# An encoder block on one core: the inverse spread over its group, norms' sums after the next projection, a fourth pair of weight buffers

## The chip, the cores and the metric

The kernel runs on one core of a Trainium2 chip. The core has TensorE (PE, matmuls, with its weight loads as PEld), VectorE (DVE), ScalarE (ACT), GpSimd (POOL) and SyncE (SP), each with its own instruction stream, and DMA queues. The metric is the device time of one execution in microseconds (us). A measurement is the median of several executions; the profile is taken on one execution of its own.

## The reference

One layer of a hybrid encoder on 512 tokens of width 1024, all in float32. The input is normalized, projected by one wide matrix, and the columns feed three token mixers: a short gated convolution (a), a gated linear recurrence (b), and RWKV-7 time mixing with 16 heads of 64 (c). Their gated sum goes through an output projection, then comes a squared-ReLU MLP of width 4096 and a last norm.

```python
h = rms_norm(x, norm1_g[l])
p = h @ w_in[l]
pa, pb, pg, pc = _split(p, (COLS_A, COLS_B, COLS_GATE, COLS_C))
...
kk = kk / jnp.maximum(jnp.sqrt(jnp.sum(kk * kk, axis=-1, keepdims=True)), 1e-12)
k = k * (1.0 + (a - 1.0) * rwkv_ka[l])
...
yc = rwkv7_recurrence(rh, decay.reshape(hs), kh, vh, kk, ah)
...
m = gate_a * y_a + gate_b * y_b + gate_c * y_c
x = x + m @ w_out[l]
h2 = rms_norm(x, norm2_g[l])
x = x + jnp.square(jax.nn.relu(h2 @ mlp_w1[l])) @ mlp_w2[l]
```

The recurrence runs over the tokens one by one in the reference. The kernel does it in 8 chunks of 64 tokens, for which it needs, per chunk and head, the inverse of a unit triangular 64 x 64 matrix.

## The kernel before

**Numbers.** A float32 operand of a large matmul is split into a high and a low part in the fp32r type: ACT casts the high part, DVE subtracts it from the source for the low part (`split_w` for weights, `split` for others, both through the helpers on lines 147 and 104). A product is then three matmuls, high x high, high x low, low x high (`mm3`, lines 168 to 170).

**Weights.** `load_w` loads 128 x 1024 weights by a DMA of SP into `raw` (2 buffers) and splits them into `whi` and `wlo`, a pair that has 3 buffers. It does so at a raised priority (`OFF`). A projection (`proj`) is 24 matmuls of 512 columns on one such pair, with a yield after each six but the last.

**Order.** The framework that builds the program orders each engine's instructions by priority (program order, unless `high_priority` raises it), with a model of their times. `keep_in_program_order` fixes an instruction's place, and `pin` raises small matmuls far up and fixes them. Each engine then runs its instructions in the order built. The waits between engines are put in by the framework. The order across stages is written by hand with generators: `weave(crit, fill, r)` runs one step of a critical generator, then r steps of a filler.

**Stages.**
- A prologue: norm sums, the first three projections on unnormalized data, `pro_scale`, which makes `hh` and `hl`.
- Four groups g of four heads each. `krv` computes k, r, v and the decays for a group: for each of two column blocks the k projection, a token shift, the squares `sq` and their split `b`, the norms' sums `pn` (two matmuls against a block matrix `bd`), `rsqrt_rows`, which makes `kk`, then the r projection and the rest. `amat` makes the chunk matrices. `inverse` makes the triangular inverses on DVE: two transposes (L551), 31 elimination steps of two operations each (a product into `dg`, an addition into `Z`), two transposes (L573), one more (L578), and then matmuls of 32 x 32 blocks, `pG` and `pT`. The inverse of group g - 1 is woven with `fill_group(g)`: 22 steps of the filler `ab`, then `krv(g)` with 16 steps of `ab` spread among its own, then 4 more. Factor `R1` sets how many filler steps go with one step of the inverse; what is left of the group runs after it. `N_TT`, `NINV` and `NG_T` are empty steps of the inverse (yields) around its transposes and small matmuls. The last inverse is woven with `ab` alone, by `R2`.
- The chain over 8 chunks (`chain`), with `ab`, `gate` and the merge of the first half (`fin_m(0, 4)`) as its filler; then `end`: `fin_m(4, 8)`. `fin_m` makes tiles `ym` in DVE, casts them on ACT and subtracts for the low part.
- The output projection, `to_tokens` (transposes `tp`, a copy `st` on DVE, a sum of squares on ACT with a scratch output `sj`), the MLP and the final norm.

`ab(q)` computes mixers a and b for one block of 128 columns: eight projections with elementwise work on DVE and ACT in between. `gate(q)` does one projection and the gate of mixer c, with a tile tagged `gc`.

Of the kernel before, what the change touches and what calls it, by code (L numbers as in the profile page):

```python
# [9 lines left out]
F32 = mybir.dt.float32  # L10
# [11 lines left out]
CP, CPV, CPI, CPC, CPN = 150, 20, 0, 20, 5  # L22
HOT = 6000

N_TT, NINV, NG_T, N_LOAD = 2, 7, 4, 6


N_KRV = 22
F_INV, F_KRV, F_GAP = 22, 16, 4
W3 = 3  # L30
R0, R1, R2, R3, R4 = 0.85, 0.87, 0.9, 1.7, 1.0
NWARM = 2
POOL_KT = (1, 3, 5, 6, 7)
S = 512
# [64 lines left out]
def block_kernel(ctx, tc, xt, win, par, mulr, sw, wout, w1, w2, fg, cst, eyes, out):  # L99
# [39 lines left out]

    def new_w():  # L140
        return (wp.tile([P, D], F32, tag="raw", name="raw", bufs=2),
                wp.tile([P, D], F32R, tag="whi", name="whi", bufs=3, align_bytes=AL),
                wp.tile([P, D], F32R, tag="wlo", name="wlo", bufs=3, align_bytes=AL))

    def split_w(w, sl):
        raw, hi, lo = w
# [40 lines left out]
            stt(t, t, -0.5, y, MUL, MUL)  # L187
            stt(y, t, 1.5, y, ADD, MUL)

    def rsqrt_rows(pool, o, ps, low, scale=1.0):  # L190

        w = pool.tile([P, S], F32, tag="rqw", name="rqw")
        q = pool.tile([P, 3, 16], F32, tag="rqq", name="rqq")
        v.transpose(w, ps)
        wv = w.rearrange("p (b j) -> p b j", j=32)[:, :, 0]
        if scale == 1.0:
            v.tensor_scalar(out=q[:, 0], in0=wv, scalar1=low, scalar2=None, op0=MAX)
        else:
            ts2(q[:, 0], wv, scale, low, MUL, ADD)
        rsqrt(q[:, 0], q[:, 1], q[:, 2])  # L200
        v.transpose(o, q[:, 1].unsqueeze(2).to_broadcast([P, 16, 32]))
# [214 lines left out]
    def krv(g, G_):  # L416
        G_.AR = pk.tile([P, 2, NC, 2, L], F32, tag="AR", name="AR")
        G_.BK = pk.tile([P, 2, NC, 2, L], F32, tag="BK", name="BK")
        vs = [p1.tile([P, S], F32, tag=f"v{h}", name=f"v{h}") for h in range(2)]
        for jj in range(2):  # L420
            j = 2 * g + jj
            rs = WP("rs")
            if j == 0:
                ks = k0
            else:
                ks = WP("ks")
                t = yield from proj(("k", j))
                shift(t, pv("mu_k", j), dvp(OMK, j), ks)
            sq = WP("a1")
            ac.activation(sq, ks, AF.Square, scale=pv("kk", j))  # L430
            sqh, sql = split(pk, sq, "b")
            pn = pm.tile([P, S], F32, tag="pm", name="pn")
            pe.matmul(pn, bd, sqh, start=True, stop=False)
            pe.matmul(pn, bd, sql, start=False, stop=True)
            kk = WP("a5")
            rsqrt_rows(pk, kk, pn, 1e-24)
            stt(kk, ks, pv("kk", j), kk, MUL, MUL)
            yield
            t = yield from proj(("r", j))
            shift(t, pv("mu_r", j), dvp(OMR, j), rs)  # L440
            yield
            swh, swl = load_sw(pk, "swa", j, 0, 2)
            pw = pm.tile([P, S], F32, tag="pm", name="pw")
            pe.matmul(pw, swh[:, 0], lws, start=True, stop=False)
            pe.matmul(pw, swl[:, 0], lws, start=False, stop=True)
            sig = WP("a1")
            ac.activation(sig, pw, AF.Tanh, bias=pv("w0", j), scale=0.5)
            v.tensor_scalar(out=sig, in0=sig, scalar1=1.0, scalar2=None, op0=ADD)
            pa = pm.tile([P, S], F32, tag="pm", name="pa")
            pe.matmul(pa, swh[:, 1], las, start=True, stop=False)  # L450
            pe.matmul(pa, swl[:, 1], las, start=False, stop=True)
            av = WP("a4")
            ac.activation(av, pa, AF.Tanh, bias=pv("a0", j), scale=0.5)
            cum = WP("a2")
            v.tensor_tensor_scan(out=cum, data0=smk, data1=sig, initial=0.0, op0=MUL, op1=ADD)
            PP = pk.tile([P, NC, L + 1], F32, tag="PPt", name="PPt")
            gp.memset(PP[:, :, 0:1], 1.0)
            Pt = PP[:, :, 1:L + 1]
            ac.activation(Pt, c3(cum), AF.Exp, scale=-0.5 * CW)
            v.tensor_copy(PL[:, g, jj], PP[:, :, L])  # L460
            pinv = WP("a3")
            ac.activation(pinv, cum, AF.Exp, scale=0.5 * CW)
            stt(G_.AR[:, jj, :, 0], c3(kk), -1.0, PP[:, :, 0:L], MUL, MUL)
            tt(G_.AR[:, jj, :, 1], c3(rs), Pt, MUL)
            t_ = WP("a1")
            stt(t_, av, 1.0, kk, ADD, MUL)
            stt(G_.BK[:, jj, :, 0], c3(t_), 0.5, c3(pinv), MUL, MUL)
            kp = WP("a2")
            ts2(kp, av, pv("ka", j), dvp(OKA, j), MUL, ADD)
            tt(kp, kp, ks, MUL)  # L470
            tt(G_.BK[:, jj, :, 1], c3(kp), c3(pinv), MUL)

            if jj == 0:
                rk = [WP(f"rk{h}") for h in range(2)]
            for h in range(2):
                r = slice(64 * h, 64 * h + 64)
                stt(rk[h][64 * jj:64 * jj + 64], rs[r], part[r, PI["rk"], j:j + 1], kp[r], MUL, MUL)

        for jj in range(2):
            for h in range(2):  # L480
                gp.dma_start(axd[:, 0:64, g, 0, 2 * h + jj].rearrange("c d t -> d c t"),
                             G_.AR[64 * h:64 * h + 64, jj, :, 0])
            gp.dma_start(rtd[:, :, g, jj].rearrange("c p t -> p c t"), G_.AR[:, jj, :, 1])
        rk = [split(pk, rk[h], ("a1", "a3") if h else "b") for h in range(2)]
        for h in range(2):
            q = 2 * g + h
            t = yield from proj(("v", q))
            shift(t, pv("mu_v", q), dvp(OMV, q), vs[h])
            yield
        for h in range(2):  # L490
            pb = pm.tile([P, S], F32, tag="pm", name="pb")
            for i in range(2):
                pe.matmul(pb, bd, rk[h][i], start=i == 0, stop=i == 1)
            BV[2 * g + h] = [bv_tile(2 * g + h, th) for th in range(2)]
            for th in range(2):
                tt(BV[2 * g + h][th], pb[:, HALF[th]], vs[h][:, HALF[th]], MUL)
        yield
        for b in range(2):
            pt = pm.tile([P, 2, 2, P], F32, tag="pm", name="pV")
            for i in range(2):  # L500
                for h in range(2):
                    pe.transpose(pt[:, i, h], vs[h][:, (2 * b + i) * P:(2 * b + i + 1) * P], ident)
            vt = p1.tile([P, 2, 2, P], F32, tag="vt", name="vt", bufs=2)
            ac.copy(vt, pt)
            for i in range(2):
                c = 2 * (2 * b + i)
                gp.dma_start(vtd[c:c + 2, :, g].rearrange("c s e v -> (c s) (e v)"),
                             vt[:, i].rearrange("p h x -> p (h x)"))
        yield
# [34 lines left out]
    def inverse(g, G_):  # L544
# [12 lines left out]
        for s in range(31):  # L557
            n, c = 31 - s, s + 1
            tv = tmp[:, 0:n * c].rearrange("l (c t) -> l c t", c=c)
            mm = tt(tv, la[:, s, s + 1:32].unsqueeze(1).to_broadcast([64, c, n]),  # L560
                    xt[:, 0:c, s:s + 1].to_broadcast([64, c, n]), MUL)
            if s % 6 == 5:

                tc.keep_in_program_order(mm)
            tt(xt[:, 0:c, s + 1:32], xt[:, 0:c, s + 1:32], tv, ADD)
            yield
# [139 lines left out]
    def fin_m(c_lo, c_hi):  # L706

        n, th = c_hi - c_lo, c_lo // 4
        for g in range(NG):
            pt = pm.tile([P, 4, P], F32, tag="pm", name="pYt")  # L710
            for i in range(n):
                pe.transpose(pt[:, i], C["Y"][:, c_lo + i, 2 * g:2 * g + 2].rearrange("p j v -> p (j v)"), ident)
            for h in range(2):
                q = 2 * g + h
                y = C["ph2"].tile([P, HT], F32, tag="ym", name="ym", bufs=2)
                tt(y.rearrange("p (c t) -> p c t", t=L), pt[:, 0:n, 64 * h:64 * h + 64],
                   GQ[q][th].rearrange("p (c t) -> p c t", t=L), MUL)
                tt(y, y, BV[q][th], ADD)
                GQ[q][th], BV[q][th] = gq_tile(q, th, F32R), bv_tile(q, th, F32R)
                ac.copy(GQ[q][th], y)  # L720
                tt(BV[q][th], y, f(GQ[q][th]), SUB)
            yield

    def gate(q):

        yc = wk.tile([P, S], F32, tag="g3", name="yc")
        gp.dma_start(yc, mpd[q])
        gt = wk.tile([P, S], F32, tag="gc", name="gc")
        t = yield from proj(("gc", q))
        ac.activation(gt, t, AF.Tanh, bias=pv("mgc", q), scale=0.5)  # L730
        swh, swl = load_sw(wk, "swc", q, 4, 1)
# [201 lines left out]
    def to_tokens(th):  # L933
        for i in (2 * th, 2 * th + 1):
            for half in range(2):
# [4 lines left out]
                st = M["xrp"].tile([P, S], F32, tag="st", name="st", bufs=2)  # L940
                v.tensor_copy(st, tp)
                gp.dma_start(x2d[i, :, half * S:(half + 1) * S], st)
                sj = M["xrp"].tile([P, S], F32, tag="sj", name="sj")
                ac.activation(sj, tp, AF.Square, accum_out=ss2[:, half, i:i + 1])
                yield

    def end():
# [181 lines left out]
```

## Time and profile before

| | us |
|---|---|
| runs shown, median of 3 (lowest to highest) | 1108.27 (1107.01 to 1110.66) |
| the profiled execution | 1108.38 |
| its span | 1106.6 |
| elimination steps of the first inverse, first to last start of `dg` | 114.2 to 155.6 |
| of the second | 234.7 to 297.9 |
| of the third | 363.1 to 412.4 |
| of the last | 485.5 to 537.0 |

In the profile an engine's busy time is the time in which it has an instruction under way. PE's matmuls are pipelined, so a PE that is busy all the time can still run below its rate: the count of matmuls in a stretch and the granted clock (PEclk) tell that. In a row of the time line the numbers are start, duration, engine, line and operation, with the idle time ahead of it and what ended it in square brackets. Rows of groups give the count, the busy time and the mean duration in ns, then the idle time ahead; rows of a tile give the count and the durations as lowest, median and highest. Rows of waits give who waited for whom, the total in us, how often, and the longest. Many elementwise operations stand on the lines of the helpers (L104, L107, L110, L147, L163), so they are told apart by their tiles.

### The profile page before, as it was taken

To read this page: it belongs to the slowest core of one execution; us is meant where nothing else is said; L and a number is where in the kernel's file an instruction comes from. 1 tells how busy PE (TensorE), PEld (TensorE's weight loads), DVE (VectorE), ACT (ScalarE), POOL (GpSimd) and SP (SyncE) were. 2 spreads that over 40 slices of the span, in tenths; PEclk is the share of its full clock that TensorE was granted. 3 is DMA by queue.
4 is the path that set the end of the run, shared out by engine and by line. 5 is a ranking of instruction groups with operands and counts; after the bars stand their busy time and mean duration, and the time that the engine had idled before them with its cause. 6 is when DMAs were issued, how large, how long until landed. Compare 5 with 4: busy or idle time off the path is not lost.

```text
span 1106.6 us, 16112 instructions
## 1 busy us (share of the span) xinstructions
PE 1056.1 (95%) x6396; PEld 865.3 (78%) x6396; DVE 743.6 (67%) x1276; ACT 473.9 (43%) x698; POOL 108.9 (10%) x167
## 2 busy tenths in 40 slices
PE   8899979999799989999899999999999999999996
PEld 5677868887588867887687887898888888888885
DVE  7997898879978998769947677955444443222224
ACT  6655445454344534534555444334433333221114
POOL 3211000210011101210022220001000000000001
PEclk9899989999989989999999999999999999999999
DMA  6243623562234623553279773234333335322231
GB/s 209 83 124 98 180 79 113 139 182 86 77 105 129 177 85 96 147 148 106 79 225 281 263 223 101 87 124 153 96 99 98 104 99 191 96 95 95 96 95 76
DMA packets 43324, 142.13 MB, mean 128 GB/s; under 512 B 5681, under 2 KB 9265, under 8 KB 42225
## 3 DMA queue, kind: packets, MB, share of 16 engines
q1 hardware_dynamic: 29472, 91.02, 25.7%
q0 software_dynamic: 13056, 49.03, 15.9%
q8 instruction: 50, 0.82, 0.3%
q10 hardware_dynamic: 720, 1.05, 0.3%
q14 instruction: 26, 0.20, 0.1%
HBM read 115.91 MB, written 25.17 MB: 127 GB/s over the span
## 4 chain that ended last, share of the span: by engine, by line
PE 65%; DVE 21%; DMA 5%; issue 5%; ACT 3%; POOL 1%; SPq 0%; ACTq 0%; POOLq 0%; DVEq 0%
PE pp L168 8%; PE pp L169 7%; PE pp L170 7%; PE acc L170 6%; PE acc L168 6%; PE acc L169 6%; PE p L169 5%; PE p L168 5%; PE p L170 5%; DVE wlo L104 4%; DMA raw<-in_win 3%; DVE dg L104 2%; DVE Z L104 2%; DMA rt<-rtd 1%; DVE u L107 1%
## 5 line engine op out<-in xcount | busy, mean ns | idle before, releaser
L104 DVE TENSOR_TENSOR wlo<-raw,whi 128x1024 fp32r<-128x1024 f32 (+1 forms) x164 | 199.5, 1219 | 249.8 <-ACT whi L147 248.9
L147 ACT CAST whi<-raw 128x1024 fp32r<-128x1024 f32 (+1 forms) x164 | 169.6, 1036 | 326.9 <-PE acc L170 125.1
L168 PE MATMUL pp<-hh,whi 128*128 128x512 f32 x696 | 278.5, 401 | 7.2 <-DVE ks L107 4.6
L170 PE MATMUL pp<-hh,wlo 128*128 128x512 f32 x696 | 277.5, 399 | 7.6 <-DVE wlo L104 7.6
L169 PE MATMUL pp<-hl,whi 128*128 128x512 f32 x696 | 277.4, 399 | 2.8 <-DVE hl L107 2.8
L168 PEld LDWEIGHTS pp<-hh,whi 128*128 128x128 f32 x696 | 133.7, 192 | 38.6 <-DVE ks L107 5.0
L170 PEld LDWEIGHTS pp<-hh,wlo 128*128 128x128 f32 x696 | 133.8, 192 | 37.6 <-DVE wlo L104 9.6
L169 PEld LDWEIGHTS pp<-hl,whi 128*128 128x128 f32 x696 | 133.7, 192 | 30.9 <-DVE hl L107 3.2
L170 PE MATMUL p<-h2h,wlo 128*128 128x512 f32 (+1 forms) x264 | 101.4, 384 | 0.0
L168 PE MATMUL p<-h2h,whi 128*128 128x512 f32 (+1 forms) x264 | 101.3, 384 | 0.0
L169 PE MATMUL p<-h2l,whi 128*128 128x512 f32 (+1 forms) x264 | 101.1, 383 | 0.0
L168 PE MATMUL acc<-whi,ah 128*128 128x512 f32 x256 | 99.6, 389 | 0.0
L169 PE MATMUL acc<-wlo,ah 128*128 128x512 f32 x256 | 99.6, 389 | 0.0
L170 PE MATMUL acc<-whi,al 128*128 128x512 f32 x256 | 99.6, 389 | 0.0
L168 PEld LDWEIGHTS p<-h2h,whi 128*128 128x128 f32 x264 | 49.7, 188 | 9.6
L170 PEld LDWEIGHTS p<-h2h,wlo 128*128 128x128 f32 x264 | 49.6, 188 | 9.7
L169 PEld LDWEIGHTS p<-h2l,whi 128*128 128x128 f32 x264 | 49.6, 188 | 9.5
L170 PEld LDWEIGHTS acc<-whi,al 128*128 128x128 f32 x256 | 48.0, 188 | 10.1
L169 PEld LDWEIGHTS acc<-wlo,ah 128*128 128x128 f32 x256 | 48.0, 188 | 10.0
L168 PEld LDWEIGHTS acc<-whi,ah 128*128 128x128 f32 x256 | 48.0, 188 | 9.8
L104 DVE TENSOR_TENSOR Z<-Z,dg 64x31 f32<-64x31 f32 (+15 forms) x124 | 42.2, 340 | 4.1
L104 DVE TENSOR_TENSOR dg<-Z 64x31 f32<-64x31 f32 (+15 forms) x124 | 42.2, 340 | 4.0
(296 smaller groups left out, 1457.0 us busy)
## 6 DMA issues: line engine op xcount, KB each, us to landing
raw<-in_win SPq DMA_DIRECT2D x88, 512.0 KB, 3.6
raw<-in_w SPq DMA_DIRECT2D x64, 512.0 KB, 3.5
ax<-axd POOLq DMA_DIRECT2D x8, 1024.0 KB, 7.2
axd<-AXt POOLq DMA_DIRECT2D x12, 512.0 KB, 7.2
bkd<-BKT POOLq DMA_DIRECT2D x4, 1024.0 KB, 13.6
raw<-in_wout SPq DMA_DIRECT2D x8, 512.0 KB, 4.3
bk<-bkd POOLq DMA_DIRECT2D x7, 512.0 KB, 8.0
swr<-in_sw SPq DMA_DIRECT2D x16, 128.0 KB, 2.3
```

The lines of the kernel that those rows point to most:

```text
L104: return v.tensor_tensor(out=o, in0=a, in1=b, op=op)
L107: return v.scalar_tensor_tensor(out=o, in0=a, scalar=s, in1=b, op0=op0, op1=op1)
L147: ac.copy(hi[:, sl], raw[:, sl])
L168: pe.matmul(ps, wh, xh, start=start, stop=False)
L169: pe.matmul(ps, wh, xl, start=False, stop=False)
L170: pe.matmul(ps, wl, xh, start=False, stop=stop)
```

## The change

Seven edits:
- The inverse's empty steps go from `N_TT, NINV, NG_T` = 2, 7, 4 to 1, 4, 3, so it yields 47 times where it yielded 54. `R1` goes from 0.87 to 1.2 and `R2` from 0.9 to 1.02.
- Every third elimination step is kept in program order, where it was every sixth.
- In `krv` the two matmuls of `pn`, `rsqrt_rows` and `kk` stand after the r projection and its shift; the square and its split stay where they were.
- `whi` and `wlo` get 4 buffers each.
- `rsqrt_rows` in `krv` uses the tile tagged `a3` for its transposed input.
- `ym` has one buffer, the gate's tile is `g1` or `g2` by turns, `sj` is gone.
- The Square of `to_tokens` is written back over its own input `tp`.

```diff
-N_TT, NINV, NG_T, N_LOAD = 2, 7, 4, 6
+N_TT, NINV, NG_T, N_LOAD = 1, 4, 3, 6
...
-R0, R1, R2, R3, R4 = 0.85, 0.87, 0.9, 1.7, 1.0
+R0, R1, R2, R3, R4 = 0.85, 1.2, 1.02, 1.7, 1.0
...
-                wp.tile([P, D], F32R, tag="whi", name="whi", bufs=3, align_bytes=AL),
-                wp.tile([P, D], F32R, tag="wlo", name="wlo", bufs=3, align_bytes=AL))
+                wp.tile([P, D], F32R, tag="whi", name="whi", bufs=4, align_bytes=AL),
+                wp.tile([P, D], F32R, tag="wlo", name="wlo", bufs=4, align_bytes=AL))
...
-    def rsqrt_rows(pool, o, ps, low, scale=1.0):
+    def rsqrt_rows(pool, o, ps, low, scale=1.0, tag="rqw"):
 
-        w = pool.tile([P, S], F32, tag="rqw", name="rqw")
+        w = pool.tile([P, S], F32, tag=tag, name="rqw")
...
             sqh, sql = split(pk, sq, "b")
+            yield
+            t = yield from proj(("r", j))
+            shift(t, pv("mu_r", j), dvp(OMR, j), rs)
             pn = pm.tile([P, S], F32, tag="pm", name="pn")
             pe.matmul(pn, bd, sqh, start=True, stop=False)
             pe.matmul(pn, bd, sql, start=False, stop=True)
             kk = WP("a5")
-            rsqrt_rows(pk, kk, pn, 1e-24)
+            rsqrt_rows(pk, kk, pn, 1e-24, tag="a3")
             stt(kk, ks, pv("kk", j), kk, MUL, MUL)
-            yield
-            t = yield from proj(("r", j))
-            shift(t, pv("mu_r", j), dvp(OMR, j), rs)
             yield
...
-            if s % 6 == 5:
+            if s % 3 == 2:
 
                 tc.keep_in_program_order(mm)
...
-                y = C["ph2"].tile([P, HT], F32, tag="ym", name="ym", bufs=2)
+                y = C["ph2"].tile([P, HT], F32, tag="ym", name="ym", bufs=1)
...
-        gt = wk.tile([P, S], F32, tag="gc", name="gc")
+        gt = W(f"g{1 + q % 2}")
...
-                sj = M["xrp"].tile([P, S], F32, tag="sj", name="sj")
-                ac.activation(sj, tp, AF.Square, accum_out=ss2[:, half, i:i + 1])
+                ac.activation(tp, tp, AF.Square, accum_out=ss2[:, half, i:i + 1])
```

## The prediction

> **What bounds the kernel now.** The first view is the page: the span, the busy time of each engine, the forty slices and the chain that ended last.
>
> ```profile
> span 1106.6 us, 16112 instructions
> PE 1056.1 (95%) x6396; PEld 865.3 (78%) x6396; DVE 743.6 (67%) x1276; ACT 473.9 (43%) x698; POOL 108.9 (10%) x167
> PE   8899979999799989999899999999999999999996
> DVE  7997898879978998769947677955444443222224
> PEclk9899989999989989999999999999999999999999
> PE 65%; DVE 21%; DMA 5%; issue 5%; ACT 3%; POOL 1%; SPq 0%; ACTq 0%; POOLq 0%; DVEq 0%
> ```
>
> PE is the resource, but VectorE holds a fifth of the chain, and the digits say where: up to slice 20 (about 560 us) PE drops below 9 in those slices in which DVE shows 8 or 9. After that PE stays full. So the second view is the table by stretches: the three whole groups, the last inverse, the chunk chain, and two stretches of 20 us. A row gives start and end, the length, the busy time of PE, of its weight loads, of DVE, ACT and POOL (instructions in brackets), the granted clock, and the DMA share and rate.
>
> ```profile
> 108.00:222.00 114.00, 108.16 (x581) 88.27 (x580) 101.45 (x184) 55.07 (x79) 13.47 (x21) 0.97 0.46 127
> 230.00:351.00 121.00, 111.56 (x582) 90.84 (x580) 102.77 (x186) 59.29 (x87) 11.85 (x18) 0.94 0.41 114
> 358.00:473.00 115.00, 109.94 (x584) 89.74 (x581) 99.61 (x180) 54.12 (x77) 13.37 (x20) 0.96 0.45 125
> 481.00:563.00 82.00, 76.39 (x436) 61.42 (x435) 69.73 (x119) 41.70 (x61) 4.69 (x7) 0.98 0.40 115
> 563.00:690.00 127.00, 124.84 (x1570) 101.19 (x1568) 85.03 (x161) 61.81 (x97) 25.61 (x48) 1.00 0.73 225
> 120.00:140.00 20.00, 20.00 (x90) 16.57 (x89) 17.03 (x32) 8.95 (x11) 0.57 (x1) 1.00 0.53 181
> 400.00:420.00 20.00, 15.41 (x59) 12.21 (x58) 19.23 (x31) 7.70 (x11) 0.00 (x0) 0.83 0.18 59
> ```
>
> The four inverse stretches (432 us) hold 373.6 us of DVE work, 86%; but it is uneven: 17.0 of 20 us in a good stretch, 19.2 in a bad one, where PE idles. The clock falls there too. The single stalls are in the time lines of PE, and the 2 to 8 us after them in the table by stretches:
>
> ```profile
> 162.15 0.80 PE L433 MATMUL pn<-bh,bd 128*128 128x512 f32 x1 [5.34 <-ACT bh L163]
> 279.40 0.79 PE L433 MATMUL pn<-bh,bd 128*128 128x512 f32 x1 [3.35 <-ACT bh L163]
> 304.82 0.80 PE L170 MATMUL pp<-hh,wlo 128*128 128x512 f32 x1 [5.82 <-DVE wlo L104]
> 408.31 0.80 PE L168 MATMUL pp<-hh,whi 128*128 128x512 f32 x1 [4.59 <-DVE ks L107]
> 523.30 0.50 PE L169 MATMUL pga<-ul,swbh 128*128 128x512 f32 x1 [1.80 <-DVE ul L104]
> 162.20:166.80 4.60, 4.60 (x11) 3.64 (x12) 4.47 (x9) 2.54 (x3) 0.00 (x0) 0.50 0.00 0
> 279.40:283.00 3.60, 3.60 (x9) 2.87 (x10) 2.78 (x6) 1.53 (x2) 0.00 (x0) 0.53 0.09 34
> 304.80:313.20 8.40, 8.38 (x75) 6.90 (x76) 7.00 (x10) 2.02 (x4) 0.00 (x0) 0.50 0.39 125
> 408.30:412.50 4.20, 4.19 (x10) 3.32 (x11) 3.94 (x9) 1.70 (x3) 0.00 (x0) 0.50 0.62 200
> 522.00:524.00 2.00, 0.70 (x3) 0.62 (x4) 1.87 (x5) 0.17 (x1) 0.00 (x0) 1.00 0.41 96
> ```
>
> The four long gaps sum to 19.1 us. After each PE runs at about half clock; the lost part is 4.6 x 0.50 + 3.6 x 0.47 + 8.4 x 0.50 + 4.2 x 0.50 = 10.3 us. The gap of 1.80 us cost no clock (1.00). So **29 us** stand to be won in the three groups.
>
> [...]
>
> **The change, part by part.**
>
> *Pace of the inverse.* An inverse is 31 elimination steps of two DVE operations, and transposes:
>
> ```profile
> L104 DVE TENSOR_TENSOR dg<-Z 64x31 f32<-64x31 f32 (+15 forms) x31 | 10.5, 340 | 1.0
> L104 DVE TENSOR_TENSOR Z<-Z,dg 64x31 f32<-64x31 f32 (+15 forms) x31 | 10.5, 340 | 1.0
> L573 DVE STREAM_TRANSPOSE Z<-Z 32x1024 f32<-32x1024 f32 x2 | 3.8, 1922 | 0.1
> L578 DVE STREAM_TRANSPOSE dg<-Z x4: 1225/1225/1226, 163.8 to 545.3; 32x1024 f32<-32x1024 f32 x4
> L551 DVE STREAM_TRANSPOSE Z<-AXt 32x1024 f32<-32x1024 f32 x2 | 4.2, 2100 | 0.0
> ```
>
> So 21.0 us of elimination, 4.2 of transposes ahead of it and 5.0 behind it. A matmul of 512 columns takes 20/90 = 0.222 us (the 90 of the stretch from 120), so a filler step of six is 1.33 us. Counted in the code, the inverse yields 54 times before and 47 after. Elimination: 31 x 0.87 = 27 filler steps (36 us of PE) before, 31 x 1.2 = 37 (49.5 us) after. The rest of a group's DVE work, 101.5 - 30.2 = 71 us, lies over some 102 us of PE (114 less the first group's 5.3 us gap, 2.3 us of clock and small stalls), a rate of 0.70. DVE demand during elimination is then 21.0/36 + 0.70 = 1.28 before and 21.0/49.5 + 0.70 = 1.12 after; the backlog by its end 0.28 x 36 = 10 us before and 0.12 x 49.5 = 6 us after. The gaps per group were 5.3, 9.2 and 4.6 us (mean 6.4), so buffers hide about 3.7 us of a backlog. After: 6 - 3.7 = 2.3 us per group by the pace alone.
>
> *Fourth pair.* The high parts wait for PE to give a buffer back:
>
> ```profile
> ACT whi L147 <- PE pp L169: 104.5, 45, 6.5
> 39.03 1.04 ACT L147 CAST whi<-raw 128x1024 fp32r<-128x1024 f32 x1 [2.10 <-PE pp L169]
> 28.66 2.29 DVE L104 TENSOR_TENSOR wlo<-raw,whi 128x1024 fp32r<-128x1024 f32 x1
> 34.36 0.79 PE L169 MATMUL pp<-hl,whi 128*128 128x512 f32 x1 [2.79 <-DVE hl L107]
> ```
>
> A fourth lets a split run up to one projection (24 x 0.222 = 5.3 us) sooner, against stalls on wlo, not on a DVE result like ks or bh. With both, 0 to 2.3 us per group are left; I take 1.3, 4 us in all: 19.1 - 4 = **-15 us** of gaps. Of the 10.3 us of clock I keep 3, since one gap may still be long: **-7 us**.
>
> In the prologue the same pair can hurt. The third stall there (2.79 us, PE on hl at 34.36) has a DVE split of 2.29 us ahead of it, where others take 1.23 (below). A split now held back to 39.03 can come before the hl parts: 0 to +2.3 us; I take **+1**. [...]
>
> *Norms' sums.* pn stood on PE ahead of the r projection and waited for shift, square and split on a full DVE. Behind r, these have 5.3 us more. That is the 5.34 and 3.35 us, already in the 15 above. In the time line of DVE:
>
> ```profile
> 155.85 1.23 DVE L104 TENSOR_TENSOR wlo<-raw,whi 128x1024 fp32r<-128x1024 f32 x1
> 163.25 0.68 DVE L104 TENSOR_TENSOR bl<-a,bh 128x512 fp32r<-128x512 f32 x1
> ```
>
> PE fell idle at 162.15 - 5.34 = 156.8. A weight split ends at 157.1, so r's matmuls have work until about 162.4; the low part bl, due at 163.9, would still come 1.5 us late on the old DVE, and in time on a less full one. The kk that comes later feeds only DVE work ahead of further projections.
>
> *Last inverse.* 31 x 0.9 = 28 filler steps become 31 x 1.02 = 32. The 1.80 us above and the 1.16 us of the row below are its stalls behind DVE: perhaps **-3**.
>
> *Tail of the inverse.* Three transposes, 5.0 us, now come in 3 x 1.2 = 3.6 steps (4.8 us) where they had 6 x 0.87 = 5.2 (7 us); backlog there (5.0/4.8 + 0.70 - 1) x 4.8 = 3.6 us against 2.9: **+2** over three groups. From the last transpose to the pinned pG there are 4 x 1.02 = 4.1 steps where 6.3 stood, in the last inverse 2.9 us less:
>
> ```profile
> 545.33 1.23 DVE L578 STREAM_TRANSPOSE dg<-Z 32x1024 f32<-32x1024 f32 x1
> 546.61 0.56 PE L585 MATMUL pG<-dg,AXt 32*32 32x32 f32 x12 [1.16 <-DVE u L789]
> 704.99 0.76 DVE L104 TENSOR_TENSOR ym<-pYt,gq 128x256 f32<-128x256 f32 x2 [0.53 <-PE pYt L712]
> 707.23 0.75 DVE L104 TENSOR_TENSOR ym<-pYt,gq 128x256 f32<-128x256 f32 x2
> L720 ACT CAST mh<-ym x16: 404/406/408, 691.1 to 713.2; 128x256 fp32r<-128x256 f32 x16
> ```
>
> pG came right behind it already, so 0 to +2.9 there; I take **+1**.
>
> *One ym.* A pair takes 707.23 - 704.99 = 2.24 us of DVE, with both halves interleaved around the ACT cast. With one buffer each half waits for its own cast, some 0.5 us: +1.0 us per pair, 4 pairs in each half of the merge. PE follows close: 0 to +6 us; I take **+2**.
>
> *At nothing:* the gate's tile in g1 or g2 (PE is full from 563 to 690 us); the Square in place on tp:
>
> ```profile
> ACT sj L944 <- DVE st L941: 5.1, 4, 2.0
> ```
>
> ACT already waits for the copy of the same tile, so nothing is serialized anew. More anchors: a rival below.
>
> Sum: -15 - 7 + 1 - 3 + 2 + 1 + 2 = -19. The profiled execution took 1108.38 us (span 1106.6 and 1.8 around it), the median of the runs is 1108.27: no correction. 1108.4 - 19 = 1089.4, **1090 us**. DVE then fills 373.6 of about 411 us, 91%, less than the 96% of its bad stretches, so it is possible.
>
> **The rivals.**
>
> *More is won.* All gaps and the half clock of the four stretches go and nothing is paid: 1108.4 - 29 - 3 = 1076. For it: backlog 6 less 3.7 less 5.3 is below nothing. Against: DVE would be busy 373.6 of 400 us, 93%, in stretches where it has lumps.
>
> *The stalls only move.* DVE has the same work, and where the load of ab and krv is lumpy PE stops at another wait instead (an AXt, a v shift, d1). Then only the two pn gaps go, half of them again lost: about 1104. For it: 71 us of other DVE work at 0.70 is a mean, and the 19.2 of 20 us from 400 show what a lump does.
>
> *Anchors hold DVE up (slower).* Every third elimination step is now kept in order, 10 per inverse for 5. DVE runs in order, so what stands behind an anchored step that stands behind an operation waiting for PE, waits too: at most one filler step, 1.33 us, mean 0.65, for 20 new anchors: 13 us. This decides if DVE's idle time per whole group grows beyond today's 12.6 to 18.2 us; with no gain it gives 1108 + 13 = 1121. Against: DVE is busy 19.2 of 20 us where PE starves, so hardly waits for PE there.
>
> **How the numbers follow.** A measurement of this kernel tells about 0.3% (3.3 us) from no change. Forecast, 1080 to 1103: 0.60. More is won, 1066 to 1080: 0.12. Stalls move, 1103 to 1112: 0.14 (0.04 below 1105, 0.10 within). Anchors or the tail, above 1112: 0.14. Faster 0.60 + 0.12 + 0.04 = 0.76, same 0.10, slower 0.14. The range 1074 to 1112 leaves out about 0.05 below and 0.14 above; the unknown costs (prologue 2.3, pG 2.9, ym 6) at their worst add 7 us to the forecast and stay in it.
>
> **What would show it.** Right: no wait of PE on bh of over 2 us; the time from the first to the last dg step in a group longer than now (41 to 63 us); DVE at 90% or more over each group; clock 0.99 in all three; whi cast less often behind PE. Wrong: a new PE wait on dg at pG; a ym wait between 690 and 715 us; a longer hl stall before 40 us; groups still 114 us long with DVE idle as before.

## The result, and the profile after

The changed kernel takes 1125.69 us (median of 4 executions, 1123.81 to 1126.38) where the kernel before took 1107.64 beside it. The ratio is 1.0153, with a 95% interval from 1.0135 to 1.0170: **slower by 18 us**, where 18 us less were forecast. The profiled execution took 1123.81 us, so the traces compare 1122.0 us of span with 1106.6.

The page of the changed kernel, in the lines that were read before:

```profile
span 1122.0 us, 16115 instructions
PE 1063.6 (95%) x6396; PEld 868.7 (77%) x6396; DVE 745.0 (66%) x1276; ACT 472.9 (42%) x698; POOL 107.9 (10%) x167
PE   8899988999999989999699998899999999999997
DVE  7997799889979898679738777765444443222223
PEclk9999999999999988999789999999999999999998
PE 56%; DVE 27%; DMA 6%; issue 6%; ACT 4%; POOL 0%; SPq 0%; DVEq 0%; ACTq 0%; POOLq 0%
```

DVE's share of the chain rose from 21% to 27%, with the same busy time. The digits show two new holes of PE: one at slice 20 (533 to 561 us, PE 6, clock 7), where the kernel before had an 8, and 8s at slices 25 and 26 (673 to 729 us), where it had 9s.

The table by stretches, cut at the first `pA` matmul of each group, at the start of the last runs of `pT`, and from the first transpose of the merge (`pYt`) to the first MLP matmul (columns as in the prediction). First the kernel before:

```profile
97.80:222.50 124.70, 116.70 (x659) 94.72 (x658) 110.64 (x197) 58.62 (x85) 15.25 (x25) 0.97 0.44 123
222.50:350.90 128.40, 118.96 (x659) 97.09 (x658) 108.39 (x195) 60.62 (x89) 11.85 (x18) 0.95 0.40 113
350.90:473.00 122.10, 117.02 (x659) 95.50 (x658) 104.97 (x188) 54.45 (x78) 14.44 (x22) 0.96 0.45 126
473.00:560.10 87.10, 81.24 (x478) 65.27 (x477) 74.96 (x126) 43.54 (x62) 4.11 (x6) 0.98 0.40 116
687.60:746.20 58.60, 54.21 (x428) 52.00 (x424) 43.16 (x92) 20.56 (x35) 2.89 (x4) 0.97 0.32 109
```

Then the changed one:

```profile
98.40:226.00 127.60, 118.25 (x660) 95.16 (x660) 110.09 (x197) 58.39 (x85) 15.09 (x25) 0.97 0.41 120
226.00:344.20 118.20, 114.22 (x659) 92.97 (x658) 105.98 (x194) 60.10 (x88) 10.55 (x17) 1.00 0.43 123
344.20:470.30 126.10, 118.61 (x659) 96.61 (x658) 104.74 (x189) 55.14 (x79) 15.35 (x24) 0.95 0.42 122
470.30:565.20 94.90, 83.42 (x472) 67.76 (x471) 75.48 (x127) 43.02 (x62) 4.10 (x6) 0.90 0.36 107
694.80:761.00 66.20, 58.06 (x423) 54.32 (x422) 45.73 (x90) 21.30 (x36) 2.87 (x4) 0.95 0.30 96
```

The three groups went from 375.2 to 371.9 us: -3.3 where -20 was expected, and only the second is better. The last inverse cost 7.8 us more (9.9 if one counts on to the merge), the merge 7.6. With 0.6 us each ahead of the first `pA` and in the MLP that is 15.4 us, all of the difference of the spans.

The time lines of PE show what it waits for now:

```profile
160.55 0.49 PE L436 MATMUL pn<-bh,bd 128*128 128x512 f32 x1 [0.95 <-ACT bh L163]
165.07 0.50 PE L450 MATMUL pa<-las,swah 128*128 128x512 f32 x1 [1.82 <-DVE rqw L194]
287.88 0.50 PE L450 MATMUL pa<-las,swah 128*128 128x512 f32 x1 [2.20 <-DVE rqw L194]
402.44 0.79 PE L168 MATMUL pp<-hh,whi 128*128 128x512 f32 x1 [5.38 <-DVE ks L107]
193.58 1.19 PE L585 MATMUL pG<-dg,AXt 32*32 32x32 f32 x32 [2.72 <-DVE dg L578]
554.93 1.27 PE L585 MATMUL pG<-dg,AXt 32*32 32x32 f32 x20 [9.18 <-DVE dg L578]
713.03 0.62 PE L168 MATMUL acc<-mh,whi 128*128 128x256 f32 x3 [0.45 <-ACT mh L720]
```

The long waits on `bh` are gone (0.95 us is left of 5.34). `pa` now waits for the PSUM buffer that `pn` holds until DVE has transposed it. The ks wait grew, and PE waits at the pinned `pG` for `L578`, by far the longest in the last inverse. In the merge PE waits 3.0 us for the first cast of `ym` (1.5 in the kernel before), and from 708 to 731 us such a wait, of 0.4 us, recurs eight times.

### The profile page after: what moved, and what is told of

Same layout as the page of the kernel before. It is cut to its first block, busy times and chain, and to the rows that moved or that the text cites. A ratio compares the mean times of both kernels' runs of the same rounds, so it can differ in the third digit from the quotient of the medians.

```text
span 1122.0 us, 16115 instructions
## 1 busy us (share of the span) xinstructions
PE 1063.6 (95%) x6396; PEld 868.7 (77%) x6396; DVE 745.0 (66%) x1276; ACT 472.9 (42%) x698; POOL 107.9 (10%) x167
## 4 chain that ended last, share of the span: by engine, by line
PE 56%; DVE 27%; DMA 6%; issue 6%; ACT 4%; POOL 0%; SPq 0%; DVEq 0%; ACTq 0%; POOLq 0%
PE acc L168 6%; PE acc L169 6%; PE acc L170 6%; PE pp L168 5%; PE pp L169 5%; PE pp L170 5%; PE p L169 5%; PE p L168 5%; PE p L170 5%; DVE wlo L104 5%; DVE dg L104 3%; DVE Z L104 3%; DMA raw<-in_win 3%; DMA rt<-rtd 2%; DVE u L107 1%
```

## The experiments

The table has, for the runs that speak on more than one stage, the length of each stage in us. The starts are read from the time lines: from the first `hh` matmul to the first `pA`, the three groups, from the last group's `pA` to the merge, and the merge. Where runs have the same code of a stage, the first stage and the first two groups agree within 0.5 us and the third group within 1.4; the groups of e3, which differs from the kernel before only in the merge, took 124.0, 130.3 and 120.9 us, up to 1.9 from those of that kernel. So differences of 2 us or less between stages carry little. e13 was profiled in its longest execution, so its stages are not compared.

The kernel before ran beside each round of experiments and took 1108.6 to 1110.6 us there, against 1107.64 beside the changed kernel; times of different rounds can be compared to some 3 us only. By their ratios to the kernel beside them, with 1.0153 for the changed kernel, the differences below stay as they are told: e1 1.0064, e2 1.0062, e4 1.0046, e5 1.0141, e6 1.0227, e10 1.0108.

| | prologue, krv 0 | group 1 | group 2 | group 3 | last inverse, chain | merge |
|---|---|---|---|---|---|---|
| before | 68.3 | 124.8 | 128.4 | 122.1 | 214.6 | 58.6 |
| changed | 71.1 | 127.6 | 118.2 | 126.1 | 224.5 | 66.2 |
| e1 last inverse old | 71.5 | 127.6 | 118.2 | 126.5 | 213.9 | 66.3 |
| e4 old pace | 71.6 | 124.2 | 124.7 | 121.4 | 215.4 | 66.2 |
| e5 three pairs | 67.8 | 128.9 | 117.8 | 129.0 | 222.0 | 67.7 |
| e6 pn at its old place | 71.6 | 129.6 | 125.1 | 129.2 | 220.9 | 66.3 |
| e10 anchors every sixth | 71.1 | 127.5 | 118.2 | 122.2 | 223.2 | 66.3 |
| e11 old pace, two ym, pair held | 67.5 | 123.7 | 126.4 | 121.4 | 213.6 | 57.9 |
| e12 as e11, second inverse at the new pace | 67.4 | 123.7 | 118.1 | 121.5 | 215.1 | 57.9 |
| e16 as e12, three pairs | 67.8 | 123.6 | 119.1 | 121.5 | 216.5 | 58.6 |

### One ym or two (e2, e3)

```diff
-                y = C["ph2"].tile([P, HT], F32, tag="ym", name="ym", bufs=1)
+                y = C["ph2"].tile([P, HT], F32, tag="Stm" if h else "ym", name="ym", bufs=1)
```

That is e2, on the changed kernel. e3 is the kernel before with `bufs=2` made `bufs=1` on this line.

> The changed kernel with a second place for ym (the second half of a pair takes the Stm slot, so two ym live at once again). Theory one-ym (each half waits for its own cast on ACT; the waits of PE on mh from 697 to 731 us come from it): first transpose of the merge to first MLP matmul falls from 66 us to about 59, time by 5 to 8 us, 1118 to 1121. Rival, the merge is late for another reason (what the chain leaves behind it, half clock): less than 2 us.

> The kernel before with ym down to one buffer and nothing else. Theory one-ym: 5 to 8 us slower than before, 1113 to 1116. Rival: within 2 us of before.

e2 took 1115.61 us: 10 under the changed kernel. e3 took 1117.22: ratio to before 1.0076 (1.0055 to 1.0098), 8 us. So one buffer costs 8 to 10 us, in either kernel, at or above the end of the 5 to 8 expected. The time line of DVE in the changed kernel shows one half of a pair:

```profile
711.12 0.43 DVE L104 TENSOR_TENSOR ml<-ym,mh 128x256 fp32r<-128x256 f32 x1 [0.47 <-ACT mh L720]
711.65 0.42 DVE L104 TENSOR_TENSOR ym<-pYt,gq 128x256 f32<-128x256 f32 x1
712.11 0.42 DVE L104 TENSOR_TENSOR ym<-ym,bv 128x256 f32<-128x256 f32 x1
713.01 0.43 DVE L104 TENSOR_TENSOR ml<-ym,mh 128x256 fp32r<-128x256 f32 x1 [0.47 <-ACT mh L720]
```

A half takes 713.01 - 711.12 = 1.89 us, a pair 3.8, where the prediction had 2.24 before and 3.2 after. The second operation now starts 0.46 us after the first, whose result it needs; with two halves taking turns two operations took 0.75 us together. In e2 the same stretch of the merge, at full clock:

```profile
695.60:752.20 56.60, 52.88 (x425) 50.88 (x423) 42.83 (x91) 21.46 (x36) 2.88 (x4) 1.00 0.34 112
```

### The last inverse (e1, e7, e8, e9, e13, e14, e15)

The new pace of the last inverse has three parts: empty steps, anchors (the steps kept in order), and R2. e1 puts all three back for this inverse alone:

```diff
     def inverse(g, G_):
+        N_TT, NINV, NG_T = (1, 4, 3) if g < NG - 1 else (2, 7, 4)
...
-            if s % 3 == 2:
+            if s % (3 if g < NG - 1 else 6) == (2 if g < NG - 1 else 5):
...
-R0, R1, R2, R3, R4 = 0.85, 1.2, 1.02, 1.7, 1.0
+R0, R1, R2, R3, R4 = 0.85, 1.2, 0.9, 1.7, 1.0
```

e7 has only the first of these edits, e8 only the second, e9 only the third; e13 the first two, e14 the first and third, e15 the last two.

> The changed kernel with the last inverse alone put back: its empty steps 2, 7, 4, every sixth step kept in order, R2 0.9. The three other inverses keep the new pace. Theory pinned (in the last inverse PE reaches the pinned pG 4.1 filler steps after the transpose L578 was placed, and DVE comes to L578 late, so PE stands 9.2 us and then runs at half clock): the pG wait falls under 2 us and the time by 7 to 11 us, to 1115 to 1119. Rival, DVE is full and the stall only moves to another wait: pG wait gone, time within 3 us of 1125.7.

> The changed kernel, with the empty steps of the last inverse alone put back to 2, 7, 4 (R2 1.02 and every third step in order stay). Theory pinned place: PE comes to pG 3 or more filler steps (4 us) later, so the wait falls from 9.2 to about 5 us or less, 3 to 5 us faster than the changed kernel. Theory anchors: elimination step 26 is still held some 12 us behind other DVE work, the wait stays over 5 us.

> The changed kernel, with every sixth elimination step of the last inverse alone kept in order (steps 1, 4, 3 and R2 1.02 stay). Theory anchors: step 26 is no longer held, the last L578 comes 8 us or more sooner, the pG wait falls under 3 us and the time by 6 to 10 us, to 1116 to 1120. Theory pinned place alone: the wait stays over 5 us, time within 3 us of 1125.7.

> The changed kernel with R2 alone put back to 0.9, which acts on the last inverse only (steps 1, 4, 3 and every third step in order stay). Theory position (with 1.02 the transposes behind the elimination come after 36.7 filler steps and so behind one more block of DVE work of ab, of some 11 us, than after the 35.1 steps of before; with 0.9 they come after 32.4): DVE needs 65 us or less from the first L551 to L578 instead of 75, the pG wait falls under 3 us, time 1115 to 1119. Rival, the shorter steps behind the elimination or the anchors do it: pG wait stays over 5 us, time within 3 us of 1125.7.

> The changed kernel, with empty steps 2, 7, 4 and every sixth step in order for the last inverse (R2 stays 1.02). In the built order DVE has 101 instructions from the last L551 to L578 (110 in the changed kernel, 101 in e1 and before), PE 276 projection matmuls from the last pA to pG (266; 246). Theory queue (PE waits at pG if the DVE work queued ahead of L578 takes longer than the matmuls queued ahead of pG): no wait over 3 us, time 1114 to 1119. Rival, R2 is needed as well: wait over 5 us, 1121 or more.

> The changed kernel, with empty steps 2, 7, 4 for the last inverse and R2 0.9 (every third step in order stays). Order: DVE 107, PE 246. Theory queue: wait 8 to 12 us, time 1121 to 1129. Rival, steps and R2 together are what e1 needed: under 3 us, 1115 to 1119.

> The changed kernel, with every sixth step in order for the last inverse and R2 0.9 (steps 1, 4, 3 stay). Order: DVE 108, PE 241. Theory queue: wait 9 to 12 us, time 1121 to 1129. Rival, anchors and R2 together are what e1 needed: under 3 us, 1115 to 1119.

| | DVE instructions, L551 to L578 | projection matmuls, last pA to pG | DVE done with L578, us | PE at pG, us | wait at the last pG, us | time, us |
|---|---|---|---|---|---|---|
| before | 101 | 246 | 73.5 | 72.4 | 1.2 | 1107.64 |
| changed | 110 | 266 | 84.5 | 75.4 | 9.2 | 1125.69 |
| e1, all three back | 101 | 246 | 73.7 | 71.1 | 2.6 | 1116.19 |
| e7, empty steps back | 110 | 276 | 84.6 | 76.1 | 8.6 | 1122.32 |
| e8, anchors back | 109 | 244 | 80.9 | 70.3 | 10.7 | 1126.17 |
| e9, R2 back | 107 | 241 | 81.6 | 69.8 | 11.8 | 1128.26 |
| e13, empty steps and anchors | 101 | 276 | 75.4 | 78.6 | none | 1117.13 |
| e14, empty steps and R2 | 107 | 246 | 81.7 | 71.8 | 10.0 | 1124.35 |
| e15, anchors and R2 | 108 | 241 | 78.9 | 70.0 | 9.0 | 1125.63 |

The first two columns come from the order in which the kernels were built, without a run; the traces of the kernel before and of the changed one have the same 101 and 110 instructions in that stretch of DVE. The next two are read from the time lines and count from the first `pA` of the last group: when `L578` ends, and when PE has done what stands ahead of `pG`. The waits are those of the rows of waits on PE; first e1, then e9 and e13:

```profile
PE pG L586 <- DVE u L790: 2.6, 1, 2.6
```

```profile
PE pG L585 <- DVE dg L578: 16.5, 3, 11.8
```

```profile
PE pG L586 <- DVE dg L579: 4.7, 2, 2.7
```

(In e13 the two waits of that row are those of the first and the third inverse; the last has none.) With all three parts put back (e1) the kernel is 9.5 us faster, as expected: this inverse is half of the loss. No part alone ends the wait, and the guesses made for e8 and e9, each that one part was the cause, fell; e7 is 3.4 us faster, as its guess of the pinned place had it, but its wait is only 0.6 shorter. What holds in all nine kernels is the comparison of the two queues: where DVE has 101 instructions ahead of `L578` the wait is small, where it has 107 to 110 it is 8.6 to 11.8 us. Waits and times of e13, e14 and e15 were forecast from these counts, and came out so. Both queues count: the time of DVE differs by up to 11 us between the kernels, that of PE by up to 9, and in e13 there is no wait because PE comes 7.5 us later than in e1, DVE only 1.7. In the changed kernel the DVE stretch reads

```profile
532.18 0.32 DVE L104 TENSOR_TENSOR Z<-Z,dg 64x156 f32<-64x156 f32 x1
...
534.58 0.69 DVE L104 TENSOR_TENSOR u<-u,g 128x512 f32<-128x512 f32 x1 [1.03 <-ACT u L781]
...
544.20 0.29 DVE L104 TENSOR_TENSOR dg<-Z 64x135 f32<-64x135 f32 x1
...
548.04 0.21 DVE L104 TENSOR_TENSOR dg<-Z 64x31 f32<-64x31 f32 x1
...
549.78 3.83 DVE L573 STREAM_TRANSPOSE Z<-Z 32x1024 f32<-32x1024 f32 x2
553.64 1.23 DVE L578 STREAM_TRANSPOSE dg<-Z 32x1024 f32<-32x1024 f32 x1
```

Elimination step 26, an anchored one, stands 12 us behind step 25: a block of `ab`'s work (two weight splits, the recurrence scan, a convolution) was put between. PE came to `pG` 3.0 us later than before, DVE was done 11.0 us later, and the wait grew by the difference, 8.0 us. Of the 11.0 us of DVE 6.7 are more work ahead of `L578`; 4.3 are more idle time (12.3 us in the stretch for 8.0), 2.5 of it in that block, where DVE waits for ACT four times. The instruction count stands for both.

And the wait is paid twice:

```profile
554.90:557.00 2.10, 2.07 (x39) 2.08 (x40) 2.06 (x3) 0.00 (x0) 0.34 (x1) 0.50 0.00 0
563.00:565.00 2.00, 2.00 (x9) 1.27 (x7) 0.55 (x1) 1.09 (x2) 0.00 (x0) 0.50 0.00 0
569.00:571.00 2.00, 2.00 (x8) 1.59 (x7) 0.00 (x0) 0.00 (x0) 0.00 (x0) 0.72 0.78 154
571.00:573.00 2.00, 2.00 (x11) 1.64 (x10) 0.63 (x1) 1.53 (x2) 0.00 (x0) 1.00 0.56 109
```

PE is busy without a break from 554.9 us on, and runs at half clock (0.50) until 570: its matmuls of 512 columns start 0.43 us apart there and 0.23 apart from 570.2 us on. By estimate, 15 us at 0.50 are some 7 us of work lost.

### The pace in the groups (e4, e10)

e4 puts the old numbers back everywhere (empty steps, R1, R2, anchors); e10 only `s % 6 == 5`.

> The changed kernel with the old pace everywhere (empty steps 2, 7, 4, R1 0.87, R2 0.9, every sixth step in order); norms' sums moved, four pairs and one ym stay. If the new pace helps in the groups and hurts only in the last inverse: about as e1 or slower, 1115 to 1122. If the new pace hurts as a whole (the anchors hold single elimination steps back by up to 22 us): faster than e1, 1105 to 1114.

> The changed kernel with every sixth elimination step kept in order in all four inverses. Read by groups, from pA to pA (changed kernel 127.6, 118.2, 126.1 us). Theory anchors hold the groups up (step 29 of the first inverse waits 22 us): the first and third group 2 us or more shorter each, the long waits of elimination steps fall on other steps. Rival, the steps' number decides nothing: groups within 1 us, time within 2 us of e8 (1126).

e4 took 1114.43 us, just under the first of the two ranges. Its three groups sum to 124.2 + 124.7 + 121.4 = 370.3 us against 371.9 with the new pace, which so gains nothing in sum: it is 6.5 us better in the second group, and 3.4 and 4.7 worse in the first and the third. e10 took 1120.22; of the groups only the third changed, by 3.9 us. So the added anchors cost the third group what it lost, and not the first, against what e10 expected of it. But e10 could not test step 29 of the first inverse: it is kept in order under either rule, and in e10 it still stands 21.7 us behind step 28.

The time line of DVE in the first inverse of the changed kernel shows why the mean rates of the prediction say so little:

```profile
161.56 0.25 DVE L104 TENSOR_TENSOR Z<-Z,dg 64x87 f32<-64x87 f32 x1
181.83 0.22 DVE L104 TENSOR_TENSOR dg<-Z 64x60 f32<-64x60 f32 x1
```

Step 29 waits 20 us. All elimination steps that start more than 5 us behind the step ahead in the changed kernel are anchored ones: 8 and 29 in the first inverse, 17 in the second, 2 in the third, 5 and 26 in the last (9.4 to 21.9 us). In the kernel before, three of the five that waited so long were anchored (11, 5 and 23, in the first three inverses); 6 and 10 in the last were not. An inverse is not spread evenly over its filler; it runs in bursts and stops, mostly at an anchor, until DVE has done what was put before that step (ahead of step 29, from 161.81 to 181.83 us, DVE is busy for 18.79 us with 38 instructions). That the anchors make these stops is argued from their places; no run was made without any.

### The fourth pair and the moved sums (e5, e6)

e5 has `bufs=3` for `whi` and `wlo` again; e6 puts the ten lines of `krv` back in their old order.

> The changed kernel with three pairs of weight buffers again, all else as changed. Theory fourth pair helps little and costs in the prologue (a split that waited now comes between the hl parts): from the first hh matmul to the first pA 68 us instead of 71, the groups 2 to 6 us longer, time within 3 us of 1125.7. Rival (as predicted): without it the groups lose 8 us or more, 1132 or above.

> The changed kernel with the norms' sums ahead of the r projection again, all else as changed. Theory move saves: the waits of PE on bh come back (3 to 5 us in the first two groups) and the waits of pa on rqw (1.8 and 2.2 us) go; 2 to 6 us slower than the changed kernel, 1128 to 1132. Rival, the stalls only moved: within 2 us of 1125.7.

e5 took 1125.35 us, the changed kernel 1125.69: the fourth pair is worth nothing in sum. The stages say that it costs 3.3 us up to the first `pA` and gives 3.8 in the groups. A place where the prediction put the cost shows in the DVE time line of the prologue of the changed kernel:

```profile
26.36 2.31 DVE L104 TENSOR_TENSOR wlo<-raw,whi 128x1024 fp32r<-128x1024 f32 x1
28.60 1.77 DVE L107 SCALAR_TENSOR_TENSOR ks<-us,mul,ks 128x511 f32<-128x511 f32 x1
30.29 3.45 DVE L107 SCALAR_TENSOR_TENSOR hl<-xT,n1t,hh 128x512 fp32r<-128x512 f32 x2
33.66 0.68 DVE L104 TENSOR_TENSOR xT<-xT,rsb 128x512 f32<-128x512 f32 x1
34.26 1.21 DVE L104 TENSOR_TENSOR wlo<-raw,whi 128x1024 fp32r<-128x1024 f32 x1
```

In the kernel before no split stands between the `hl` parts from 31 to 38 us; here one comes at 34.26. It takes only 1.21 us. PE stands 5.6 us in this stage for 3.9 in e5, so its waits are 1.7 of the 3.3 us; the rest is not traced. With one pair held back until the `hl` parts are made (e11, below) the stage takes 67.5 us, so the cost is the pair's.

e6 took 1134.58 us, 9 more than the changed kernel and 2 over what was expected, all of it in the groups (383.9 us against 371.9). The old waits are back:

```profile
162.79 0.79 PE L433 MATMUL pn<-bh,bd 128*128 128x512 f32 x1 [4.83 <-ACT bh L163]
444.34 0.50 PE L433 MATMUL pn<-bh,bd 128*128 128x512 f32 x1 [3.77 <-ACT bh L163]
```

The move of the sums is the part of the change that pays, but what it pays hangs on the pace. The three groups take 375.3 us with the old pace and the old place (the kernel before), 383.9 with the new pace and the old place (e6), 370.3 with the old pace and the new place (e4), 371.9 with both new. So the move is worth 12 us at the new pace and at most 5 at the old one (e4 has the fourth pair too, the kernel before has not), and the new pace without the move costs some 9.

### A version that beats both (e11, e12, e16)

e11 is the changed kernel with the old pace, e2's two `ym`, and one of the four pairs kept out of use through the prologue:

```diff
+    hold = [wp.tile([P, D], F32R, tag=t, name="hold", bufs=4, align_bytes=AL) for t in ("whi", "wlo")]
+    for t in hold:
+        gp.memset(f(t)[:, 0:1], 0.0)
     wlr = [new_w()]
...
         pro_scale()
+    for i, t in enumerate(hold):
+        gp.tensor_tensor(out=hs_[:, i:i + 1], in0=f(t)[:, 0:1], in1=f(hl[:, KT - 2 + i])[:, 0:1], op=MUL)
```

e12 adds the new pace for the second inverse alone; e16 is e12 with three pairs and no hold.

```diff
-R0, R1, R2, R3, R4 = 0.85, 0.87, 0.9, 1.7, 1.0
+R0, R1, R2, R3, R4 = 0.85, (0.87, 1.2, 0.87), 0.9, 1.7, 1.0
...
     def inverse(g, G_):
+        N_TT, NINV, NG_T = (1, 4, 3) if g == 1 else (2, 7, 4)
...
-            if s % 6 == 5:
+            if s % (3 if g == 1 else 6) == (2 if g == 1 else 5):
...
-            weave(inverse(g - 1, GS[g - 1]), fgr, R1, CPV)
+            weave(inverse(g - 1, GS[g - 1]), fgr, R1[g - 1], CPV)
```

> Norms' sums moved and four pairs, with the old pace, two ym (as in e2), and one of the four pairs kept out of use until the last hl part of the prologue is made (a small GpSimd product reads it then). If the terms add up: e4 1114.4, less 8.5 for ym, less 3 for the prologue: 1103, 5 us under before. If the fourth pair's gain in the groups needs the early start: 1105 to 1107.

> As e11, with the new pace (steps 1, 4, 3, every third step in order, filler factor 1.2) for the second inverse only, whose group was 118.2 us with it and 124.7 without. If a group's time depends on its own inverse's pace: 6 us under e11, about 1097. If the gain there was only the other side of the first group's loss: within 2 us of e11.

> e12 with three pairs of weight buffers and without the hold in the prologue. If the fourth pair gives in the groups what e5 against the changed kernel showed (4 us, paid back by 3.3 us in the prologue that e12 does not pay): 1101 to 1104. If it gives nothing here: within 2 us of e12 (1098.5).

e11 took 1104.52 us, ratio to before 0.9954 (0.9940 to 0.9967). e12 took 1098.54, ratio 0.9899 (0.9886 to 0.9912); its second group was 118.1 us beside a first of 123.7, so the gain there stands on that inverse's own pace. e16 took 1096.57, ratio 0.9892 (0.9878 to 0.9907): with three pairs it is as fast, so a fourth pair is not needed. e16's first, third and last inverse have the old pace. Its trace has the clock at 0.983 for 0.978 before, and no wait of PE over 2.8 us but one on ks:

```profile
span 1096.7 us, 16114 instructions
PE 1054.3 (96%) x6396; PEld 862.5 (79%) x6396; DVE 740.4 (68%) x1276; ACT 473.3 (43%) x698; POOL 107.8 (10%) x167
```

## Why the prediction was wrong

The reading of the bound was right: up to 560 us PE stands behind DVE, and after each of its six stalls of over 3 us there (four in the kernel before, two in the changed one, 3.35 to 9.18 us) the granted clock was 0.50 to 0.53. That a stall of 1.8 us keeps the clock was one case and no rule (last section). The -7 us of clock took it that a stall cut short gives its clock back; the traces show that for the second group, where the longest wait fell from 5.82 to 2.20 us and the clock went from 0.95 to 1.00. The first stayed at 0.97 (1.00 behind the 1.82 us at 165.07 us, but 0.50 behind 2.72 us at `pG`, from 194.67 to 201.50 us), and the third, with 5.38 us on ks, went from 0.96 to 0.95. The terms, by the prediction's own steps:

- **Pace of the inverse and fourth pair, -15 and -7.** This step failed. Its working was a mean rate: DVE demand per filler step, 1.28 before and 1.12 after, and a backlog from the difference. (Its 102 us of PE should be 106, 114 less 5.8 idle and 2.3 of clock, which makes both demands 0.03 less and is not the reason.) The traces show an inverse that runs in bursts, so the mean has no stretch in which it holds. The elimination did not get longer everywhere: 41 to 69, 63 to 49, 49 to 52, 52 to 65 us. The groups gained 3.3 us in all, less than the moved sums alone are worth (e6: 12 us in the groups), and e4 shows that pace gained nothing; with the sums at their old place it cost some 9 us (e6).
- **Fourth pair.** Mis-sized on both sides: the cost in the prologue was 3.3 us (taken 1, at most 2.3, the price of one split, which took 1.21 us), the gain in the groups 3.8 us, the sum nothing (e5).
- **Norms' sums.** Right in the mechanism: waits on `bh` fell from 5.34 and 3.35 to 0.95 and none in these two places, and the old waits come back with the old order (e6). The move alone did not do it in the first group: with the old pace (e4) PE still waits 3.38 us on `bh` there. A new one was not foreseen: `pa` waits 1.8 to 2.2 us for the PSUM buffer that `pn` holds.
- **Last inverse, -3, and pG, +1.** This step failed, and it is half of the loss. The price of `pG` was worked out as the shift of PE's place in filler steps (2.9 us at most). What decides is when DVE comes to `L578`, against when PE comes to `pG`: DVE's stretch grew by 11 us (from the first L551 to L578: 64 to 75 us), PE's by 3. The wait was named among the things that would prove the forecast wrong; its price was read from the wrong queue.
- **One ym, +2.** The mechanism was right, the size was not: 8 to 10 us (e2, e3). The prediction's own 1.0 us for each of 8 pairs is 8 us of DVE; it took 2, as if PE hid the rest, and PE hid little. A pair lost 1.5 us of overlap and not 1.0, and beside the waits of PE on `mh` the granted clock was 0.83 from 700 to 720 us, where e2 has 1.00 over its merge.
- **Rivals.** That the stalls only move was the nearest of them for the groups. The anchors came to the slower side: every sixth instead of every third is worth some 5 us in the changed kernel (e10). But the mechanism was another: DVE's idle time did not grow (51.1 us over the three groups, 51.2 before); the inverse comes late.

One thing stays open: why the first group is 3.4 us longer with the new pace. It was not the added anchors (e10). PE stands 9.4 us in it for 6.9 in e4, so 2.5 us are waits (2.7 at `pG` and 1.8 at `pa`, where e4 has the 3.38 on `bh`). What brings `pG` there so late, the stop at step 29 perhaps, was not tried. Nor was it tried whether the wait of `pa` goes if `pn` gets another buffer.

## What to carry to other kernels

Where one engine's instruction is put early in its queue by hand, what it costs is read by comparing two queues: the work ahead of it there, and the work ahead of its producer on the other engine; here both were counted in the built order, and the counts forecast three runs. A buffer taken from a step in which two engines take turns on the same data cost the overlap of the turns here, 1.5 us for each of 8 pairs of tiles, and the bound engine paid most of it (8 to 10 us, e2 and e3). A change with several parts has to be tried part by part, and the parts together too: taken out of the changed kernel, one part was worth 9 us, two nothing, and two cost 9 us each, but the one that paid was worth at most 5 at the old pace.

## What the runs showed of the hardware

After the wait of 9.2 us PE stayed at half clock (0.50) for 15 us although it was busy all the time. In these 15 us stand 64 matmuls `pG` and 64 `pT` of 32 x 32 blocks, in three bursts of 3.6, 1.9 and 1.9 us, between matmuls of 512 columns. In the kernel before, after a gap of 4.6 us with no such burst behind it, half clock lasted 4.2 us from PE's next matmul on. The next rows show such places; the first four are of the kernel before, the last two of e16. In a row of a stretch the third number from the end is the granted clock.

```profile
436.46:439.87 3.41, 3.41 (x69) 2.87 (x69) 1.79 (x8) 0.62 (x2) 0.00 (x0) 1.00 0.22 82
439.87:443.28 3.41, 3.41 (x9) 2.67 (x10) 2.50 (x9) 1.66 (x3) 0.71 (x1) 0.50 0.38 74
546.61 2.21 PE L585 MATMUL pG<-dg,AXt 32*32 32x32 f32 x64 [1.16 <-DVE u L789]
549.10:552.51 3.41, 3.41 (x10) 2.63 (x9) 3.31 (x5) 0.93 (x1) 0.00 (x0) 0.50 0.33 74
511.42 0.50 PE L169 MATMUL pga<-ul,swbh 128*128 128x512 f32 x1 [1.80 <-DVE ul L104]
512.43:515.84 3.41, 3.41 (x9) 2.63 (x8) 3.21 (x7) 2.01 (x3) 0.00 (x0) 0.50 0.19 79
```

From 436.46 to 439.87 us PE has no idle time, but 2.3 us of it are two bursts of 32 `pT`; the next 3.41 us run at half clock. At 549.1 us half clock follows a wait of 1.16 us and a burst of 64 `pG`. The wait of 1.80 us on `ul` that kept the clock in the kernel before (at 523.30 us, 1.00) is followed by half clock in e16 (0.50 from 512.43 us), with no burst near; so is a wait of 1.81 us at 537.93 us of the changed kernel (0.50 from 539.42 to 542.83 us), while after 2.20 us at 287.88 us of the same kernel the clock stayed at 1.00. So the length of a wait alone does not tell whether the clock falls.

But for the one at the kernel's end, the stretches at half clock in the traces of the kernel before and of the changed one last 3.41 us (six of them), 6.83 (seven), 10.24 and 20.48 us. Not each has a long wait just ahead of it: for the one at 539.42 us of the changed kernel it was 1.81 us, and ahead of the one at 439.87 us of the kernel before PE was busy for 3.41 us. Whether the bursts of 32 x 32 matmuls have a part in it is not shown; no run was made for it.
